# A decoder layer on one core: first down-projection operands in residual buffers, spilled residual tiles first, and the compressed branch of four heads in one exponential

## The chip, the cores and the metric

The kernel runs on one core of a Trainium2 chip. Its engines are TensorE (PE: matmuls; PEld: their weight loads), VectorE (DVE), ScalarE (ACT), GpSimd (POOL) and SyncE (SP), which issues most of the DMAs. The metric is the device time of one execution in microseconds.

## The reference

One layer over x of 1024 tokens by 1024 columns, in float32:

```
h = rms_norm(x, g_mix_norm);  z = h @ w_in            # q, 6 x k/v, gates, 3 x conv columns
per token block, kv group and head, in three branches (compressed, selected, window):
    p = masked_softmax(q.k - slope*dist);  o_branch = p @ v
attn_out = sum over branches of gate_branch * o_branch
conv_out = b_gate * conv3(c_gate * h_conv)
x = x + concat(rms_norm(attn_out), rms_norm(conv_out)) @ w_o
x = x + square(relu(rms_norm(x) @ w_up)) @ w_down     # 4096 hidden columns
```

There are 8 heads of 64 columns in 2 groups g of 4. A softmax is exp(s - max)/sum over the keys of its branch; the compressed branch has 64 keys. A float32 product is computed as three products of high and low parts (`mm3`: high·high, low·high, high·low), so each operand is split into a rounded part and the rest of it (`split`; from PSUM `split_psum`).

## The kernel before

The program first records every operation, and a planner orders them: `schedule` (L339) walks the recorded operations with estimated costs of each engine and gives every engine its own list, in which an operation with a long remaining chain goes ahead of one that was written earlier. A written-out loop is thus no order of execution, but it decides which buffers (and so which waits) an operation has. As one helper issues everything, all instructions of the profile have line L268; they are told apart by the names of their tiles.

Stages, in us of the profiled execution. **0 to 150**: norm and projections. **150 to 282**: the conv columns (`zc` banks); DVE makes the conv result `cv`, which is split into `MCh` and `MCl`, and the sums of its squares, `sqs`. Eight small matmuls `s__` of `sqs` with ones (L1013 on) then give the norm's factor `rconv`.

**282 to 340**: conv half of the output projection. The loop at L1030 goes over the eight blocks of 128 tokens in the order ORDER = 3, 2, 1, 0, 4, 5, 7, 6. For each it loads the residual of x, makes two banks `wc` of 12 matmuls and adds them, scaled by `rconv`, on DVE. The first six residual tiles stay in the ring "y" of six buffers. The last two (tokens 7 and 6) have no buffer there: they use the one buffer `xt`, which lies where `sqs` lay, and are stored to DRAM (`x1_d`) by a DMA that POOL issues. Among these matmuls stand transposes of the keys (`tp<-ident,kn`, L1028) and the queries (`qx` loaded by SP, `tpq`, `Qg`, `Qz`) and scores of the first token block.

**340 to 650**: attention, 16 pairs of token block and group. `scores` (L930) makes a head's scores in PSUM; DVE adds the distance penalty while it writes them out (`pc` for the compressed branch, `pt` for the others) and takes the extreme `nm`; ACT takes the exponential and its sum `sm`, for each head and branch in an instruction of its own; `rr` is gate over sum. `weigh` (L1073) transposes the probabilities, splits them (`ph`, `pl`) and multiplies by the values into `ot`. For each branch, in the order 1, 2, 0 (selected, window, compressed), `tail` (L1098) copies `ot` to `oTs` (ACT), transposes back into `ops` (PE), multiplies by `rr` into `ot_s` (DVE) and adds to the output `osb` (POOL). `finish` (L1146) does the attention half of the output projection (`wa` banks) and stores the sum to `x2_d`.

**650 to 957**: the up-projection in 16 pairs of hidden blocks (`pair`, L1356), by a Strassen scheme of 7 products. The squared results `d` (a tile of two halves, also in the ring "y") are put into DRAM tiles `u_d` by SP.

**957 to the end**: down-projection, L1457 on, in 8 chunks c of 2 pairs each; for a product p of 7 it loads `ur` from `u_d` (two, one for each pair), splits it into `uu` (high by ACT, low by DVE or POOL), combines and splits the weights (`we`), and runs 24 matmuls into 4 banks `X` (p = 0 to 3 accumulate in them). After each p DVE adds the four banks to residual tiles `y` in SBUF, which for chunk 0 are loaded from `x2_d` at L1475. So a matmul of p = 1 into bank `X` comes after the add of p = 0, and this after the load of `y`. The pools of `ur`, `uu` and `y` (L1432 to L1434) lie in space that the up stage's pools give back at L1429.

Of the kernel before, what the change touches and what calls it, by code (L numbers as in the profile page):

```python
# [9 lines left out]
F32 = mybir.dt.float32  # L10
F32R = mybir.dt.float32r
# [483 lines left out]
def trunk_layer(ctx, tc, x, g_mix_norm, w_in, g_q, g_k, pe_cmp, w_cmp1, b_cmp1, w_cmp2, b_cmp2,  # L495
# [341 lines left out]
    with ExitStack() as b2:  # L837
# [92 lines left out]
        def scores(tb, g, Qt, filler):  # L930
            Qg, Qz = Qt
            W = (tb + 1) * P
            WW = min(W, 640)
            nm = st.tile([P, 3, R], F32, name="nm")
            sm = st.tile([P, 3, R], F32, name="sm")
            pc = pts[g].tile([P, R, NCMP], F32, name="pc", bufs=1)
            Ps = []
            k_w = NCMP + T + W - WW
            N = NCMP + W
            cuts = [N] if N <= 512 else [320, N] if N <= 640 else [N - 512, N] if N <= 1024 else [320, N - 512, N]  # L940
            pieces = []
            c0 = 0
            for c1 in cuts:
                parts = [] if c0 else [(0, 0, NCMP, 0)]
                o = max(c0, NCMP)
                parts.append((1, o - NCMP, c1 - o, o - c0))
                pieces.append((c0, c1 - c0, parts))
                c0 = c1
            if WW == 640:
                pieces.append((k_w + 384, 256, [(2, 384, 256, 0)]))  # L950
                pieces.append((k_w, 384, [(2, 0, 384, 0)]))
            else:
                pieces.append((k_w, WW, [(2, 0, WW, 0)]))
            banks = []
            for k, n, parts in pieces:
                m = max(n, 256)
                for bank in banks:
                    if bank[0] + m <= 512:
                        break
                else:  # L960
                    bank = [0, []]
                    banks.append(bank)
                bank[1].append((k, m, bank[0], parts))
                bank[0] += m
            dtile = {0: (d_c, 56 - 8 * tb), 2: (d_sw, 512 + 640 - WW), 1: (d_sw, T - W)}
            for sl, r in enumerate(HEADS):
                sc = -(2.0 ** -(g * R + r + 1))
                pt = pts[g].tile([P, 640 + T], F32, name="pt", bufs=R)
                Ps.append(pt)
                dst = {0: pc[:, r], 2: pt[:, 0:WW], 1: pt[:, 640:640 + W]}  # L970
                seen = set()
                for _, group in banks:
                    s_ = psS.tile([P, 512], F32, name="s_")
                    for k, m, s0, _ in group:
                        nc.tensor.matmul(s_[:, s0:s0 + m], Qg[:, r], KH[g][:, k:k + m], start=True, stop=False)
                        nc.tensor.matmul(s_[:, s0:s0 + m], Qz[:, r], KL[:, k:k + m], start=False, stop=True)
                    for k, m, s0, parts in group:
                        for b, off, n, x in parts:
                            dd, d0 = dtile[b]
                            if b == 1 and d0 + off >= 512:  # L980
                                d0 += P
                            acc = nm[:, b, sl:sl + 1]
                            nc.vector.tensor_tensor_reduce(out=dst[b][:, off:off + n], in0=s_[:, s0 + x:s0 + x + n],
                                                           in1=dd[:, d0 + off:d0 + off + n],
                                                           scale=sc, scalar=acc if b in seen else 1e20,
                                                           op0=ALU.add, op1=ALU.min, accum_out=acc)
                            seen.add(b)
                for b in (1, 2, 0):
                    nc.scalar.activation(dst[b], dst[b], AF.Exp, bias=nm[:, b, sl:sl + 1],
                                         scale=-1.0, accum_out=sm[:, b, sl:sl + 1])  # L990
                for _ in range(-(-len(filler) // (R - sl))):
                    filler.pop(0)()
            rr = st.tile([P, 3, R], F32, name="rr")
            nc.vector.scalar_tensor_tensor(rr, sm, 1e-30, gates[:, tb, g], op0=ALU.max, op1=ALU.mult)
            nc.vector.reciprocal(rr, rr)
            return (Ps, pc), rr
# [30 lines left out]
        kts = [(i % 2, i // 2 % 2, i // 4) for i in range(8)]  # L1027
        for i in range(4):  # L1028
            k_transposes(*kts.pop(0))
        for it, tb in enumerate(ORDER):  # L1030
            xt = xq.tile([P, D], F32, name="xt") if it >= 6 else y_tile([P, D], f"y{tb}")
            nc.sync.dma_start(xt, x2d[tb * P:(tb + 1) * P])
            t = slice(tb * P, (tb + 1) * P)
            for nh in range(2):
                n = slice(nh * 512, (nh + 1) * 512)
                tag, bufs = (("ot", 2), ("ot", 2), ("ms", 1))[(it * 2 + nh) % 3]
                ps = psC.tile([P, 512], F32, name="wc", tag=tag, bufs=bufs)
                for c in range(4):
                    wh, wl = pieces[c]
                    mm3(ps, MCh[:, c, t], MCl[:, c, t], wh[:, 0, n], wl[:, 0, n], c == 0, c == 3)  # L1040
                nc.vector.scalar_tensor_tensor(xt[:, n], ps, rconv[:, tb:tb + 1], xt[:, n],
                                               op0=ALU.mult, op1=ALU.add)
            if it < 6:
                yacc[tb] = xt
            else:
                nc.gpsimd.dma_start(x1_d[tb * P:(tb + 1) * P], xt)
            for i in range(2):
                if kts:
                    k_transposes(*kts.pop(0))
            if it == 3:  # L1050
                Qn = queries(ORDER[0])
                first = scores(ORDER[0], 0, Qn[0], [])
# [4 lines left out]
    with ExitStack() as c_:  # L1057
# [15 lines left out]
        def weigh(tb, g, probs, rr, osb):  # L1073
# [24 lines left out]
            def tail(ot, b):  # L1098
                oTs = pq.tile([P, 512], F32, name="oTs", bufs=2)
                copy_act(oTs, ot[0])  # L1100
                ops = psC.tile([P, R, 2, HD], F32, name="ops", tag="ms", bufs=1)
                for r in range(R):
                    nc.tensor.transpose(ops[:, r].rearrange("p a d -> p (a d)"), oTs[:, r * P:(r + 1) * P], ident)
                t = pq.tile([P, R, 2, HD], F32, name="ot_s", bufs=2)
                c = rr[:, b].unsqueeze(2).unsqueeze(3).to_broadcast([P, R, 2, HD])
                tt(nc.vector, t, ops, c, ALU.mult)
                tv = t.rearrange("p (j i) a d -> p j i a d", j=2)
                if b == 1:
                    tt(nc.gpsimd, og, tv[:, :, :, 0], tv[:, :, :, 1], ALU.add)
                else:  # L1110
                    for k in range(2):
                        tt(nc.gpsimd, og, og, tv[:, :, :, k], ALU.add)
# [344 lines left out]
    for c in range(NPAIR // CHUNK):  # L1457
# [6 lines left out]
        for p in range(7):  # L1464
            ops = []
            for i, q in enumerate(qs):
                ur = eu.tile([P, 512], F32, name="ur", bufs=8)
                nc.sync.dma_start(ur, u_d[q][p])
                u = split([eU.tile([P, 512], F32R, name="uu", tag=f"u{h}", bufs=10) for h in "hl"], ur,
                          nc.gpsimd if i else nc.vector)  # L1470
                w = split(w_unit(), down_comb(Bs[i], WANT[p]), nc.vector if i else nc.gpsimd)
                ops.append((u, w))
            if c == 0 and p in (0, 1):
                for tb in range(TH[p] * 4, TH[p] * 4 + 4):
                    nc.sync.dma_start(yacc[tb], x2_d[tb * P:(tb + 1) * P])  # L1475
            ih, n = ACC[p]
            for j in range(4):
                if p == 0:
                    X[j] = bank_p("X") if j < 3 else bank_1("X")
                elif p in (4, 6):  # L1480
                    X[j] = bank_d("Z") if j % 2 else bank_e("Z")
                t = slice(j * P, (j + 1) * P)
                for i, ((uh, ul), (wh, wl)) in enumerate(ops):
                    mm3(X[j], uh[:, t], ul[:, t], wh, wl, i == 0 and p in (0, 4, 6), i == CHUNK - 1, skip_group_check=True)
                tb = TH[ih] * 4 + j
                y = yacc[tb][:, n * 512:(n + 1) * 512]
                tt(nc.vector, y, X[j], y, ALU.add)
                if c == NPAIR // CHUNK - 1 and p >= 3:
                    nc.sync.dma_start(out2d[tb * P:(tb + 1) * P, n * 512:(n + 1) * 512], y)
# [29 lines left out]
```

## Time and profile before

| | |
|---|---|
| three runs | 1276.68, 1278.77, 1284.4 us; median 1278.77 |
| the profiled execution | 1283.21 us; its span 1281.1 us, mean granted TensorE clock 0.994 |
| PE busy | 1241.3 us, 97% of the span |
| DVE, ACT, POOL busy | 896.0, 691.0, 680.0 us |

The profiled execution's own time is 2.1 us over its span. The engines' busy times overlap, so their shares don't add up to the span. The granted clock of a stretch is a mean over it: 1.00 is 2.4 GHz all the time, 0.50 would be 1.2 GHz all the time. In a list of instructions, the brackets give the engine's idle time before one and what ended it.

### The profile page before, as it was taken

Reading aid. Unit: us, or ns where it says so; the run is one execution under the profiler, and the core shown is the slowest. Engines: PE = TensorE matmul, PEld = TensorE weight load, DVE = VectorE, ACT = ScalarE, POOL = GpSimd, SP = SyncE. Lnnn points to the kernel's source line nnn. Section 1 sums busy time; section 2 is a strip of 40 time slices with the busy share of each in tenths; the row PEclk is TensorE's granted clock in tenths of the full one; section 3 lists DMA queues with packets and bytes.
Section 4 is the critical chain, followed back from the end, with each engine's and each line's share of the span. In section 5 each row is a group of like instructions: output and inputs, shape, how many; then the busy total and the mean of one; then the engine's idle time right before and its main releaser. Section 6 shows DMA issues by size and latency. Waiting matters only on the chain.

```text
span 1281.1 us, 18498 instructions
## 1 busy us (share of the span) xinstructions
PE 1241.3 (97%) x6170; PEld 1028.4 (80%) x6170; DVE 896.0 (70%) x1805; ACT 691.0 (54%) x1514; POOL 680.0 (53%) x599
## 2 busy tenths in 40 slices
PE   7999999999999999999899999999999999999998
PEld 6898888888778888888778888888877787888786
DVE  6357874333588788988884656555657988888874
ACT  7345552111589888887956455555444444444440
POOL 2245512120133422211676777777887989878860
PEclk9999999999999999999999999999999999999999
DMA  6243441202320110000315445345339655544413
GB/s 233 76 123 118 132 117 49 81 26 82 99 83 34 39 45 18 26 18 17 116 56 183 131 149 172 115 162 176 133 136 377 201 173 164 164 144 131 138 42 131
DMA packets 91575, 147.68 MB, mean 115 GB/s; under 512 B 10900, under 2 KB 45800, under 8 KB 91480
## 3 DMA queue, kind: packets, MB, share of 16 engines
q1 hardware_dynamic: 88408, 138.70, 33.7%
q10 hardware_dynamic: 2304, 5.24, 1.1%
q0 software_dynamic: 768, 2.56, 0.6%
q8 instruction: 49, 0.80, 0.3%
q14 instruction: 46, 0.38, 0.1%
HBM read 102.43 MB, written 44.04 MB: 114 GB/s over the span
## 4 chain that ended last, share of the span: by engine, by line
PE 83%; DVE 5%; DMA 4%; ACT 4%; issue 2%; POOL 1%; DVEq 0%; ACTq 0%; SPq 0%; POOLq 0%
PE X L268 23%; PE Z L268 15%; PE zc L268 10%; PE zp L268 8%; PE tp L268 6%; PE ot L268 5%; PE wa L268 3%; PE wc L268 3%; PE W L268 3%; DMA wu<-in_w_up_dram 2%; PE ops L268 1%; DVE y L268 1%; PE hp L268 1%; ACT wu L268 1%; DVE we L268 1%
## 5 line engine op out<-in xcount | busy, mean ns | idle before, releaser
L268 PE MATMUL X<-we,uu 128*128 128x512 f32 x768 | 193.1, 393 | 5.9 <-ACT uu L268 5.0
L268 PEld LDWEIGHTS X<-we,uu 128*128 128x128 f32 x768 | 144.6, 189 | 39.3 <-ACT uu L268 8.3
L268 PE MATMUL Z<-we,uu 128*128 128x512 f32 x576 | 147.6, 391 | 0.6 <-DVE y L268 0.6
L268 ACT ACTIVATE uu<-ur 128x512 fp32r<-128x512 f32 x112 | 68.9, 629 | 124.9 <-PE X L268 62.2
L268 PEld LDWEIGHTS Z<-we,uu 128*128 128x128 f32 x576 | 107.3, 188 | 26.0 <-DVE y L268 2.4
L268 PE MATMUL tp<-ident,pt 128*128 128x128 f32 x528 | 101.4, 275 | 2.3 <-ACT pt L268 1.3
L268 POOL TENSOR_TENSOR d<-d 128x512 f32<-128x512 f32 x64 | 96.3, 1525 | 12.5 <-DVE d L268 11.3
L268 DVE TENSOR_TENSOR pl<-tp,ph 128x512 fp32r<-128x512 f32 (+1 forms) x148 | 95.2, 655 | 7.5 <-ACT ph L268 7.1
L268 ACT ACTIVATE pt<-pt,nm 128x640 f32<-128x640 f32 (+7 forms) x128 | 93.8, 736 | 9.8 <-DVE nm L268 9.5
L268 ACT ACTIVATE ph<-tp 128x512 fp32r<-128x512 f32 (+1 forms) x148 | 82.9, 575 | 20.5 <-PE tp L268 14.9
L268 DVE TENSOR_TENSOR y<-X,y 128x512 f32<-128x512 f32 x128 | 79.6, 681 | 15.8 <-PE X L268 15.3
L268 ACT ACTIVATE w_hi<-w_raw,cols 128x128 fp32r<-128x128 f32 (+3 forms) x128 | 54.0, 486 | 67.4 <-PE zc L268 48.9
L268 POOL TENSOR_TENSOR uu<-ur,uu 128x512 fp32r<-128x512 f32 x56 | 78.2, 1401 | 15.2 <-DVE y L268 10.7
L268 DVE TENSOR_TENSOR we<-s,we 128x512 fp32r<-128x512 f32 x42 | 39.2, 934 | 60.0 <-ACT we L268 27.3
L268 DVE TENSOR_TENSOR uu<-ur,uu 128x512 fp32r<-128x512 f32 x56 | 65.7, 1178 | 20.7 <-ACT uu L268 19.8
L268 PEld LDWEIGHTS tp<-ident,pt 128*128 128x128 f32 x528 | 68.6, 141 | 13.6 <-ACT pt L268 2.7
L268 DVE SCALAR_TENSOR_TENSOR w_lo<-w_raw,cols,w_hi 128x128 fp32r<-128x128 f32 (+3 forms) x128 | 61.5, 525 | 24.1 <-ACT w_hi L268 23.8
L268 DVE TENSOR_TENSOR y<-Z,y 128x512 f32<-128x512 f32 x96 | 61.4, 684 | 23.7 <-PE Z L268 23.7
L268 ACT ACTIVATE wu<-wu,cols 128x256 f32<-128x256 f32 x128 | 55.4, 501 | 23.4 <-DMA wu<-in_w_up_dram 21.4
L268 POOL TENSOR_TENSOR osb<-osb,ot_s 128x256 f32<-128x256 f32 x64 | 49.2, 769 | 34.7 <-DVE ot_s L268 30.1
L268 ACT ACTIVATE we<-wu 128x512 fp32r<-128x512 f32 x57 | 35.6, 630 | 58.7 <-PE X L268 45.8
L268 PE MATMUL zc<-hTl,w_hi 128*128 128x512 f32 x192 | 65.3, 389 | 0.0
(1261 smaller groups left out, 3588.4 us busy)
## 6 DMA issues: line engine op xcount, KB each, us to landing
u_d<-d SPq DMA_DIRECT2D x112, 256.0 KB, 4.1
ur<-u_d SPq DMA_DIRECT2D x112, 256.0 KB, 2.7
wu<-in_w_up_dram SPq DMA_DIRECT2D x16, 1024.0 KB, 5.5
wd<-in_w_down_dram SPq DMA_DIRECT2D x16, 1024.0 KB, 5.8
w_raw<-in_w_in_dram SPq DMA_DIRECT2D x20, 512.0 KB, 4.0
xt<-in_x_dram SPq DMA_DIRECT2D x10, 512.0 KB, 5.2
w_raw<-in_w_cmp_dram SPq DMA_DIRECT2D x8, 512.0 KB, 4.1
q_d<-qn SPq DMA_DIRECT2D x8, 512.0 KB, 2.9
```

Source lines behind the costliest of these rows:

```text
L268: node.do.append(lambda: getattr(engine, method)(*[real(x) for x in a], **{k: real(x) for k, x in kw.items()}))
```

## The change

Three edits. First, in chunk 0 the loaded operands of p = 0 and p = 1 get other tiles: `uf`, a tile of two halves, of which the second takes the load and then the low part, the first the high part. For p = 0 these lie in the slots "x" of the pools yl and e1 (which hold weights or residual tiles earlier), for p = 1 in the ring "y". Second, the loop at L1030 takes the two blocks with the tile `xt` first, then the six others. Third, in `scores` the compressed branch leaves the loop over heads: POOL subtracts the scores of four heads from the extreme, ACT takes one exponential over 256 columns without a sum, and DVE reduces to the four sums; in `tail` for that branch ACT copies `ops` to `ot_s`, and POOL adds the two halves, multiplies by `rr` and adds to `osb`.

```diff
@@ scores
-                for b in (1, 2, 0):
+                for b in (1, 2):
                     nc.scalar.activation(dst[b], dst[b], AF.Exp, bias=nm[:, b, sl:sl + 1],
                                          scale=-1.0, accum_out=sm[:, b, sl:sl + 1])
...
+            order = "p (j i) -> p i j"
+            mx = nm[:, 0].rearrange(order, j=2).unsqueeze(3).to_broadcast([P, 2, 2, NCMP])
+            pv = pc.rearrange("p (i j) n -> p i j n", j=2)
+            tt(nc.gpsimd, pv, mx, pv, ALU.subtract)
+            nc.scalar.activation(pc, pc, AF.Exp)
+            nc.vector.tensor_reduce(sm[:, 0].rearrange(order, j=2), pv, axis=AX.X, op=ALU.add)
             rr = st.tile([P, 3, R], F32, name="rr")
@@ conv half of the output projection
-        for it, tb in enumerate(ORDER):
+        for it, tb in [*enumerate(ORDER)][6:] + [*enumerate(ORDER)][:6]:
@@ tail
                 t = pq.tile([P, R, 2, HD], F32, name="ot_s", bufs=2)
+                tv = t.rearrange("p (j i) a d -> p j i a d", j=2)
+                if b in (0,9):
+                    copy_act(t, ops)
+                    tt(nc.gpsimd, tv[:, :, :, 0], tv[:, :, :, 0], tv[:, :, :, 1], ALU.add)
+                    c = rr[:, b].rearrange("p (j i) -> p j i", j=2).unsqueeze(3).to_broadcast([P, 2, 2, HD])
+                    tt(nc.gpsimd, tv[:, :, :, 0], tv[:, :, :, 0], c, ALU.mult)
+                    tt(nc.gpsimd, og, og, tv[:, :, :, 0], ALU.add)
+                    return
@@ down-projection
-                ur = eu.tile([P, 512], F32, name="ur", bufs=8)
+                if c == 0 and p < 2:
+                    both = (y_tile([P, 2, 512], "uf") if p else (yl, e1)[i].tile([P, 2, 512], F32, name="uf", tag="x")).bitcast(F32R)
+                    u, ur = [both[:, 0], both[:, 1]], both[:, 1].bitcast(F32)
+                else:
+                    u = [eU.tile([P, 512], F32R, name="uu", tag=f"u{h}", bufs=10) for h in "hl"]
+                    ur = eu.tile([P, 512], F32, name="ur", bufs=8)
                 nc.sync.dma_start(ur, u_d[q][p])
-                u = split([eU.tile([P, 512], F32R, name="uu", tag=f"u{h}", bufs=10) for h in "hl"], ur,
-                          nc.gpsimd if i else nc.vector)
+                split(u, ur, nc.gpsimd if i else nc.vector)
```

How the planner's lists change at three places. SP's list around the boundary from up to down (`u_d_204` and `u_d_203` are the DRAM tiles of the first two pairs, `u_d_190` and `u_d_189` those of the last two, `x_d` here is `x2_d`). Before:

```order
L268 DMA u_d_189<-d 128x512
L268 DMA u_d_190<-d 128x512
L268 DMA u_d_189<-d 128x512
L268 DMA ur<-u_d_204 128x512
L268 DMA ur<-u_d_203 128x512
L268 DMA y_10073<-x_d 128x1024
L268 DMA y_10072<-x_d 128x1024
L268 DMA y_10071<-x_d 128x1024
L268 DMA y_10070<-x_d 128x1024
L268 DMA ur<-u_d_204 128x512
L268 DMA ur<-u_d_203 128x512
```

And after the change:

```order
L268 DMA u_d_190<-d 128x512 x6
L268 DMA uf<-u_d_204 128x512
L268 DMA u_d_190<-d 128x512
L268 DMA u_d_189<-d 128x512
L268 DMA uf<-u_d_203 128x512
L268 DMA y_10084<-x_d 128x1024
L268 DMA y_10083<-x_d 128x1024
L268 DMA y_10082<-x_d 128x1024
L268 DMA y_10081<-x_d 128x1024
L268 DMA ur<-u_d_204 128x512
L268 DMA ur<-u_d_203 128x512
```

The loads for p = 1 stand among the last puts of the up stage (those for p = 0 far up in the list, behind the first put of each of the first two pairs), and nothing stands between them and the loads of `y`. DVE's list at the start of the conv half of the output projection. Before:

```order
L268 TENSOR_TENSOR cv<-cv 128x512
L268 TENSOR_TENSOR sqs_1968<-sqs_1968,cv 128x512
L268 TENSOR_TENSOR KL<-tp,KH_2793 64x512
L268 TENSOR_SCALAR rs_t<-s__2825 128x8
L268 TENSOR_TENSOR KL<-tp,KH_2792 64x512
L268 TENSOR_TENSOR KL<-tp,KH_2793 64x512
L268 SCALAR_TENSOR_TENSOR y_2622<-wc,rconv,y_2622 128x512 x2
L268 SCALAR_TENSOR_TENSOR y_2801<-wc,rconv,y_2801 128x512
```

And after:

```order
L268 TENSOR_TENSOR cv<-cv 128x512
L268 TENSOR_TENSOR sqs_1968<-sqs_1968,cv 128x512
L268 TENSOR_SCALAR rs_t<-s__2825 128x8
L268 SCALAR_TENSOR_TENSOR xt<-wc,rconv,xt 128x512 x2
L268 TENSOR_TENSOR KL<-tp,KH_2793 64x512
L268 TENSOR_TENSOR KL<-tp,KH_2792 64x512
L268 TENSOR_TENSOR KL<-tp,KH_2793 64x512
L268 SCALAR_TENSOR_TENSOR y_2622<-wc,rconv,y_2622 128x512
L268 TENSOR_TENSOR KL<-tp,KH_2792 64x512
L268 TENSOR_TENSOR KL<-tp,KH_2793 64x512
L268 SCALAR_TENSOR_TENSOR xt<-wc,rconv,xt 128x512 x2
```

The adds to the first `xt` tile stand directly behind `rs_t` (which leads to `rconv`), ahead of three `KL`; those to the second come after two more `KL`. POOL's list at the first pairs of the attention. Before:

```order
L268 COPY Qz<-Qg 64x512
L268 MEMSET Qz 64x512
L268 TENSOR_TENSOR osb<-ot_s 128x2x2x64
L268 TENSOR_TENSOR osb<-osb,ot_s 128x2x2x64 x4
L268 TENSOR_TENSOR osb<-ot_s 128x2x2x64
```

And after:

```order
L268 TENSOR_TENSOR pc<-nm,pc 128x256
L268 COPY Qz<-Qg 64x512
L268 TENSOR_TENSOR osb<-ot_s 128x2x2x64
L268 MEMSET Qz 64x512
L268 TENSOR_TENSOR osb<-osb,ot_s 128x2x2x64 x2
L268 TENSOR_TENSOR ot_s<-ot_s 128x4x64
L268 TENSOR_TENSOR ot_s<-ot_s,rr 128x4x64
L268 TENSOR_TENSOR osb<-osb,ot_s 128x2x2x64
```

The subtraction for the next pair stands ahead of the current pair's sums, and the compressed branch's last two adds became three operations, of which the second needs `rr`.

## Rows read from the trace of the kernel before

**Rows 1.** The page's first part: busy time of each engine, share of the span and number of instructions.

```profile
PE 1241.3 (97%) x6170; PEld 1028.4 (80%) x6170; DVE 896.0 (70%) x1805; ACT 691.0 (54%) x1514; POOL 680.0 (53%) x599
```

**Rows 2.** Windows of the conv half's start and end and of the attention: the stretch, its length, busy time (and instructions) of PE, PEld, DVE, ACT and POOL, the granted clock, the DMA engines' share and GB/s.

```profile
290.00:295.00 5.00, 5.00 (x25) 4.37 (x26) 0.86 (x2) 1.18 (x3) 1.65 (x1) 0.69 0.63 197
340.00:345.00 5.00, 2.85 (x15) 2.30 (x14) 2.14 (x11) 2.84 (x6) 1.15 (x3) 0.81 0.61 211
345.00:350.00 5.00, 5.00 (x28) 4.40 (x28) 3.87 (x13) 4.75 (x12) 0.00 (x0) 0.85 0.37 109
350.00:630.00 280.00, 271.74 (x1710) 229.09 (x1708) 242.29 (x769) 242.81 (x622) 83.97 (x122) 1.00 0.13 45
```

**Rows 3.** The chain of waits from the last up matmul to p = 1: start, duration, what.

```profile
957.09 2.87 DMA ur<-u_d
...
959.99 0.64 ACT uu L268
...
960.67 7.33 PE X L268 x24
...
968.09 0.63 ACT we L268
...
969.29 5.73 PE X L268 x24
```

**Rows 4.** The same view later in the down-projection: 24 matmuls of one product without a break.

```profile
1015.71 5.44 PE X L268 x24
```

**Rows 5.** The window behind the boundary, with the columns of rows 2.

```profile
960.00:965.00 5.00, 4.33 (x12) 3.45 (x13) 1.44 (x2) 1.25 (x2) 5.00 (x4) 0.66 0.99 379
```

**Rows 6.** The tile `y` from 955 to 975: instructions with the duration of one in ns (least, median, most) and the first and last start; then the time from the issue of a load to its landing.

```profile
L268 SPq DMA_DIRECT2D y<-x_d x8: 319/351/647, 958.1 to 967.3; - x8
L268 DVE TENSOR_TENSOR y<-X,y x6: 680/682/692, 966.9 to 974.8; 128x512 f32<-128x512 f32 x6
...
DMA to landing us min/median/max: 7.9/8.3/8.8
```

**Rows 7.** SP's queue there: start and duration of the issues.

```profile
957.09 0.90 SPq L268 DMA_DIRECT2D ur<-u_d  x2
958.08 2.02 SPq L268 DMA_DIRECT2D y<-x_d  x4
```

**Rows 8.** The tile `xt` from 280 to 345, as in rows 6.

```profile
L268 DVE SCALAR_TENSOR_TENSOR xt<-wc,rconv,xt x4: 743/748/751, 327.4 to 338.7; 128x512 f32<-128x512 f32 x4
...
DMA to landing us min/median/max: 3.4/3.7/4.0
```

**Rows 9.** The timeline at the store of the first `xt` tile and the load of the second.

```profile
329.42 0.64 POOL L268 DMA_DIRECT2D x_d<-xt  x1 [5.58 <-DVE nm L268]
...
333.52 0.33 SPq L268 DMA_DIRECT2D xt<-in_x_dram  x1
```

**Rows 10.** The timeline at the start of the conv half of the output projection.

```profile
281.75 0.70 PE L268 MATMUL wc<-w_hi,MCh 128*128 128x512 f32 x2
...
287.65 0.69 DVE L268 TENSOR_TENSOR sqs<-sqs,cv 128x512 f32<-128x512 f32 x1
...
288.99 0.55 PE L268 MATMUL tp<-ident,kn 128*128 128x128 f32 x3 [0.68 <-DVE KL L268]
289.37 0.95 PE L268 MATMUL s__2825<-ones,sqs 128*128 128x1 f32 x8
...
296.21 1.04 PE L268 MATMUL tp<-ident,kn 128*128 128x128 f32 x8
```

**Rows 11.** The timeline of PE at its end.

```profile
342.02 0.63 PE L268 MATMUL tpq<-ident,qx 128*128 128x128 f32 x4 [1.41 <-DMA qx<-q_d]
343.40 1.11 PE L268 MATMUL tp<-ident,pt 128*128 128x128 f32 x4 [0.75 <-ACT Qg L268]
```

**Rows 12.** The groups of instructions from 340 to 660, each shape apart: busy time, mean ns of one, and the idle time before them with what ended it.

```profile
L268 PE MATMUL tp<-ident,pt 128*128 128x128 f32 x523 | 100.8, 275 | 2.3 <-ACT pt L268 1.3 <-ACT Qg L268 0.7
...
L268 POOL TENSOR_TENSOR osb<-osb,ot_s 128x256 f32<-128x256 f32 x64 | 49.2, 769 | 34.7 <-DVE ot_s L268 30.1 <-DVE rr L268 1.3 <-DVE nm L268 0.7
L268 PE MATMUL ops<-ident,oTs 128*128 128x128 f32 x192 | 36.1, 277 | 2.9 <-ACT oTs L268 1.9 <-DVE ot_s L268 0.9
...
L268 DVE TENSOR_TENSOR ot_s<-ops,rr 128x512 f32<-128x512 f32 x48 | 32.9, 685 | 4.3 <-PE ops L268 3.4 <-POOL Qz L268 0.2 <-POOL osb L268 0.2
...
L268 ACT ACTIVATE oTs<-ot 128x512 f32<-128x512 f32 x48 | 28.5, 598 | 4.8 <-PE ot L268 4.3
...
L268 ACT ACTIVATE pc<-pc,nm 128x64 f32<-128x64 f32 x60 | 20.8, 348 | 0.3 <-DVE nm L268 0.2
...
L268 ACT ACTIVATION_READ_ACCUMULATOR pc<-pc,nm 128x1 f32 x60 | 12.0, 200 | 0.0
...
L268 DVE TENSOR_TENSOR pl<-tp,ph 128x256 fp32r<-128x256 f32 x16 | 6.7, 421 | 0.1
...
L268 ACT ACTIVATE ph<-tp 128x256 fp32r<-128x256 f32 x16 | 6.2, 385 | 0.9 <-PE tp L268 0.9
...
L268 DVE SCALAR_TENSOR_TENSOR rr<-sm,gates 128x12 f32<-128x12 f32 x16 | 3.7, 230 | 1.1 <-ACT pt L268 1.1
```

**Rows 13.** The timeline of PE in chunk 0 of the down-projection: the two runs that waited for DVE.

```profile
998.59 5.88 PE L268 MATMUL Z<-we,uu 128*128 128x512 f32 x24 [0.42 <-DVE y L268]
...
1009.31 3.00 PE L268 MATMUL X<-we,uu 128*128 128x512 f32 x12 [0.53 <-DVE y L268]
```

More of the change, by code (lines that the diff above doesn't have):

```diff
@@ L1104, in tail @@
                 t = pq.tile([P, R, 2, HD], F32, name="ot_s", bufs=2)
+                tv = t.rearrange("p (j i) a d -> p j i a d", j=2)
[6 more added lines that the diff above has]
+                    return
                 c = rr[:, b].unsqueeze(2).unsqueeze(3).to_broadcast([P, R, 2, HD])
                 tt(nc.vector, t, ops, c, ALU.mult)
-                tv = t.rearrange("p (j i) a d -> p j i a d", j=2)
                 if b == 1:
```

## The prediction

> **What bounds the kernel now.** I first read the busy shares of the engines: TensorE (PE) works 1241.3 of the 1281.1 us span, 97%, and no other engine passes 70% [rows 1]. So time can come only from matmuls taken away, and the change takes none; from stretches in which PE stands idle; and from stretches in which its clock is low. The sum of all idle time is 40 us, and the question is how much of it the three edits can reach. Next come the windows of the stages the edits touch [rows 2]. In the attention stretch, 350 to 630 us, PE has 271.74 of 280, idle 8.26; ScalarE (ACT) has 242.8 and VectorE (DVE) 242.3, both below PE. In the windows around the conv half of the output projection the granted clock is 0.69 (290 to 295), 0.81 and 0.85 (340 to 350), a mixture of the levels 1.2 and 2.4 GHz. Then the chain of waits between up- and down-projection [rows 3], the one place where PE provably waits for what the first edit moves.
>
> The profiled execution took 1283.21 us; the median shown is 1278.77. I sum against 1283.21 and scale by 1278.77/1283.21 at the end.
>
> **Edit 1, first down operands, gain 3.** Before, the first u tile is loaded only when the up stage's space is free: 2.87 us of load from 957.09, 0.64 of ACT for its high part, and the first down matmul at 960.67 [rows 3]. A full-clock run of 24 such matmuls takes 5.44 [rows 4], 0.2266 each; this first run took 7.33 [rows 3], in a window with clock 0.66 [rows 5]: 1.89 lost. Then PE waits for ACT's `we`, whose issue waited for that run's start, and p=1 begins at 969.29.
>
> After, both operand pairs are loaded during the up stage, so p=0 can follow the last up matmul at about 957.5 and end at 957.5+5.44 = 963.0. But p=1 writes the bank that DVE adds to `y` after p=0, and `y` is loaded only when the space opens, at about 957.3. Before, this gate was hidden: the first `y` row came 7.9 us after its issue and the add ran at 966.9, less than 2.4 ahead of p=1 [rows 6]. After, the four `y` loads stand first on SP's queue, two `ur` loads earlier than before (the order of SP); issue times of before are 957.09 for `ur` and 958.08 for `y` [rows 7]. The nearest price for a load that is ahead of the traffic is that of `xt`, the same 512 KB, 3.4 to 4.0 [rows 8]; the nearest in this company is `y`'s own 7.9 [rows 6]. So y0 lands between 957.3+3.7 = 961.0 and 957.3+7.9 = 965.2, plus 0.68 for the add: p=1 starts between 963.0 (no wait at all) and 965.9, against 969.29. That is 6.3 to 3.4 gained. Where PE then idles 2.9 the clock may fall as it did before [rows 5], 1.9 back: 1.5 to 6.3. I take 3, nearer to `y`'s own row, since the eight `y` loads still go out together with `ur`, in a window that moves 379 GB/s [rows 5].
>
> The Trainium skill says otherwise: its page "DMA: Bandwidth & Descriptors", section "Queues, rings and completion order", gives each issuing engine's queue its own rings, in which descriptors start in order, so that what is queued behind a load should not delay it. By that rule the first `y` row would land early and the whole 6.3 would come (rival C). This trace speaks rather against it: `y`, queued behind 0.5 MB, took 7.9 or more [rows 6], where 0.5 MB at 379 GB/s [rows 5] is 1.3 us beyond `xt`'s 3.7, 5.0 in all.
>
> What the tiles cost: they lie in residual and D tiles that are free by then. The p=0 loads stand behind the first puts of the first two pairs, almost the whole up stage ahead of their use. The second p=1 load stands behind puts of pair 15 and directly ahead of `y`. Splits are the same instructions, earlier, on DVE and POOL. Zero.
>
> **Edit 2, tokens of the spilled tiles first, gain 2.8.** At the end of the conv half, the spilled tiles' reload and store no longer collide with the next query load: PE's waits 1.41 for `qx` and 0.75 for `Qg` [rows 11] go, 2.16, and with them the low clock. From 340 to 350 the clock cost between 0.15·5 = 0.75 and 0.19·5+0.75 = 1.7 [rows 2]; I take 1.2. Together −3.4.
>
> At the front, now: 0.68 idle before the key transposes [rows 10] and 0.31·5 = 1.55 by the clock [rows 2], 2.2 in all. After: PE runs the first 24 matmuls from 281.75 to 287.2; then the small `s__` sums need `sqs`, which DVE ends at 288.34 [rows 10]: 1.1 idle. The `xt` tile lies in the space of `sqs`, so its load cannot go before these sums, about 289.3: +3.7 (the median of its loads [rows 8]) + 0.75 for the add [rows 8] = 293.8; PE, with 12 matmuls (2.72) and 12 transposes (1.56 from 1.04 for 8 [rows 10]), is there at 293.6: 0.2 idle. The second tile's load waits for the store of the first: 294.5, store to reload 4.1 (329.42 to 333.52 [rows 9]), 298.6, +3.7+0.75 = 303.1; PE has 34 matmuls and 12 transposes left from 293.8, 9.3: 303.1, no idle. With the same dip of 1.55: 2.9, so +0.6. Sum −2.8; bounds −3.5 (no idle in front), and +9.4 where the two loads cost `y`'s 7.9 and bring two more dips.
>
> **Edit 3, one exponential for four heads, gain 2.** ACT loses 64 exponentials of 0.348 and 64 reads of the accumulator of 0.200, 35.1; it gains 16 of the 256-column kind, 0.385 by `ph`, and 16 copies from PSUM, 0.598 by `oTs` [rows 12]: 15.7. That is 19.4 less of 242.8 [rows 2]. DVE loses 16 multiplications of 0.685 and gains 16 reductions over 256 columns; a reduction isn't in the trace, so 0.21 (half the `pl` row) to 0.42 (the row itself): at 0.42, 4.3 less. POOL gains 32 operations of 0.769 [rows 12], 24.6 on 84.0 busy of 280 [rows 2]: covered, unless one stands in a chain (rival A). Since PE has no fewer matmuls, the gain is bounded by its idle time, 8.26; only part of its waits is on ACT (2.9 before `ops`, 2.3 before `tp`, over 340 to 660), so I take a quarter, 2; bounds −8.3 and, by rival A, +16.
>
> **Later.** Two small waits for DVE's add, 0.42 and 0.53 [rows 13], stand in chunk 0, in which the early splits leave DVE room: I take half, 0.5.
>
> Sum: −3 −2.8 −2 −0.5 = −8.3, 1274.9 beside 1283.21, **1270.5** by the median.
>
> **Rivals.**
> A, slower: the compressed chain grows. `rr`, which every tail of all branches needs, now waits for POOL's subtraction, the common exponential and a reduction, 0.77+0.39+0.42 = 1.58, where one head's exponential and read, 0.55, came last: 1.0 more in each of 16 (block, group) pairs, 16 on the path, and the 2 don't come: 1270.5+18 = 1288.5. It decides if `rr` comes later than the first tail (branch 1) wants it. For: POOL may be busy with the other pair's sums then. Against: `rr` waited only 1.1 on ACT in the whole stage [rows 12], and a pair holds some 17 us of PE work (280/16) in between. 0.12.
> B: the front of edit 2 stands in loads of 7.9 instead of 3.7: 8.4 idle and dips, 12.2 against the forecast: 1282.7. It decides if store plus load pass the 9.3 of work there. For: the clock dip at 290 coincides with 197 GB/s [rows 2]. Against: the price of store to reload is from the same pair of tiles. 0.13.
> C: `y` rows land in order and early, p=1 doesn't wait: 3.3 more, 1267; with more of the attention's idle time, 1263 to 1266. 0.15.
> D: the clock falls again at p=1 and ACT's relief lies beside matmuls: edits 1 and 3 give 1.5 and 0, 1274 to 1276. 0.10.
> Forecast, 1266 to 1274: 0.50.
>
> **Numbers.** One per cent (about what a measurement of this kernel can tell from no change) is 12.8 us: faster means below 1266.0, slower above 1291.6. Below 1266.0: half of C and a little of the forecast's edge, 0.14; above 1291.6: A with a mishap, 0.03; within: 0.83. The range from C's end to B's, 1263 to 1283, leaves out A, the tail of C and unnamed cases.
>
> **What would show it.** Right: the first down matmul within 1 us of the last up matmul; p=1's first wait on DVE's `y`, ending 5.5 to 8.5 us after the last up matmul; no wait for `qx` where the conv half ends; ACT near 223 and POOL near 109 busy in the attention's 280 us, PE idle there 5 to 7. Wrong: `ops` or `ot_s` waiting on `rr` (A); PE waits over 3 us on DVE's `xt` (B); p=1 right behind p=0 (C); a clock below 0.9 behind the boundary and 8 us idle in the attention (D).

## The result, and the profile after

The changed kernel takes 1264.51 us (median of 6 runs, 1262.25 to 1266.38) beside 1277.61 of the kernel before: ratio 0.9889, interval 0.9866 to 0.9911, faster by 13.1 us by the medians and by 14.2 by the ratio. The forecast was 1270.5, range 1263 to 1283. So the direction and the range held, and the size was low: the time is the one that rival C gave with more of the attention's idle time, 1263 to 1266, and it lies below 1266.0, which had a chance of 0.14.

The profiled execution fell from 1283.21 to 1264.10, by 19 us, more than the medians: that execution of the kernel before was 5.6 above its median, and it had low clock at 75 to 80, 290 to 295 and 340 to 350 us, where the new one has none (more on this below).

The page's first part, which answers to [rows 1]:

```profile
PE 1234.4 (98%) x6170; PEld 1023.4 (81%) x6170; DVE 902.1 (71%) x1805; ACT 683.1 (54%) x1418; POOL 708.5 (56%) x631
```

The same number of matmuls; ACT has 96 records fewer and POOL 32 more.

**The boundary.** Four views of the changed kernel there, for [rows 3, 6, 7]: the chain of waits (one row holds the last up matmul, all of p = 0 and p = 1 and the start of p = 2), PE's timeline, SP's and DVE's timelines with, in brackets, the idle time and its releaser, and the landing times of `y`.

```profile
946.83 13.38 PE X L268 x56
```

```profile
947.12 11.57 PE L268 MATMUL X<-we,uf 128*128 128x512 f32 x48
```

```profile
947.09 1.74 SPq L268 DMA_DIRECT2D y<-x_d  x4
948.88 1.25 SPq L268 DMA_DIRECT2D ur<-u_d  x2
```

```profile
951.82 1.29 DVE L268 TENSOR_TENSOR y<-X,y 128x512 f32<-128x512 f32 x2 [0.43 <-PE X L268]
...
955.58 1.89 DVE L268 TENSOR_TENSOR y<-X,y 128x512 f32<-128x512 f32 x3 [0.44 <-DMA y<-x_d]
```

```profile
DMA to landing us min/median/max: 6.3/6.7/7.1
```

48 matmuls of two products run without a break, directly behind the last up matmul. The first `y` is issued at 947.09, and its add starts at 951.82: so the load was there at most 4.7 us after its issue. And the add waited 0.43 for PE, not for the load: in the order of PE's list the first bank gets its last matmul of p = 0 as the 19th of 24, which ends at 947.12 + 18 x 0.2266 + 0.39 = 951.6. Only the fourth add waits for its load, 0.44. The view's landing times (6.3 at least) can't hold for the first tile, so they don't tell when a single tile was there; an add that ran, or waited, does.

**The conv half's start**, for [rows 8, 10]: windows, PE's timeline and the landing of `xt`.

```profile
290.00:295.00 5.00, 4.75 (x26) 3.87 (x24) 3.38 (x5) 1.69 (x3) 0.64 (x1) 1.00 0.26 105
```

```profile
291.24 0.50 PE L268 MATMUL wc<-w_hi,MCh 128*128 128x512 f32 x1 [0.25 <-DVE xt L268]
```

```profile
DMA to landing us min/median/max: 2.9/2.9/3.0
```

The whole price of the moved `xt` loads is 0.25 us of idle time, and the waits of [rows 11] are gone.

**Idle time of PE by stage.** Of every kernel, two windows of nearly the same work: the 100 us from the first conv matmul `wc`, and from there to the last `wa` matmul (columns of [rows 2]). Before and after:

```profile
281.70:381.70 100.00, 94.00 (x500) 77.32 (x499) 63.08 (x169) 50.89 (x130) 23.60 (x34) 0.97 0.30 93
381.70:650.00 268.30, 260.37 (x1626) 219.42 (x1625) 226.82 (x703) 228.68 (x576) 91.47 (x121) 1.00 0.11 37
```

```profile
279.10:379.10 100.00, 96.61 (x524) 78.71 (x523) 66.92 (x180) 50.60 (x116) 27.75 (x39) 1.00 0.28 93
379.10:637.40 258.30, 253.11 (x1594) 214.63 (x1593) 217.49 (x692) 219.77 (x492) 106.03 (x147) 1.00 0.11 39
```

Idle in the first window 6.0 and 3.4, in the second 7.9 and 5.2. (The second holds the first matmuls of the up-projection too.) The third stage is from the last up matmul to the end of the span: 1281.1 − 957.5 = 323.6 before and 1262.3 − 947.1 = 315.2 after. I use these three numbers for every experiment.

### The profile page after: what moved, and what is told of

It is laid out like the page before. It is cut to its first block, busy times and chain, and to the rows that moved or that the text cites. A ratio compares the mean times of both kernels' runs of the same rounds, so it can differ in the third digit from the quotient of the medians.

```text
span 1262.3 us, 18410 instructions
## 1 busy us (share of the span) xinstructions
PE 1234.4 (98%) x6170; PEld 1023.4 (81%) x6170; DVE 902.1 (71%) x1805; ACT 683.1 (54%) x1418; POOL 708.5 (56%) x631
## 4 chain that ended last, share of the span: by engine, by line
PE 87%; DMA 4%; ACT 4%; DVE 3%; issue 1%; SPq 0%; POOL 0%; ACTq 0%; DVEq 0%; POOLq 0%
PE X L268 24%; PE Z L268 16%; PE zc L268 10%; PE zp L268 8%; PE tp L268 6%; PE ot L268 5%; PE wa L268 4%; PE W L268 3%; PE wc L268 3%; DMA wu<-in_w_up_dram 2%; PE ops L268 1%; DVE we L268 1%; PE hp L268 1%; DVE y L268 1%; ACT wu L268 1%
## 5 line engine op out<-in xcount | busy, mean ns | idle before, releaser
L268 PE MATMUL X<-we,uu 128*128 128x512 f32 x720 | 179.2, 390 | 1.6 <-DVE y L268 1.5
L268 PEld LDWEIGHTS X<-we,uu 128*128 128x128 f32 x720 | 134.5, 188 | 31.5 <-ACT uu L268 2.2
L268 DVE TENSOR_TENSOR y<-X,y 128x512 f32<-128x512 f32 x128 | 79.8, 681 | 13.7 <-PE X L268 13.0
L268 DVE TENSOR_TENSOR uu<-ur,uu 128x512 fp32r<-128x512 f32 x54 | 69.2, 1293 | 12.5 <-ACT uu L268 11.4
L268 PEld LDWEIGHTS tp<-ident,pt 128*128 128x128 f32 x528 | 67.8, 140 | 11.8 <-PE s__4915 L268 0.6
L268 DVE TENSOR_TENSOR y<-Z,y 128x512 f32<-128x512 f32 x96 | 61.3, 683 | 21.1 <-PE Z L268 21.1
L268 PE MATMUL zc<-hTh,w_lo 128*128 128x512 f32 x192 | 65.1, 390 | 0.0
```

Source lines behind the costliest of these rows:

```text
L268: node.do.append(lambda: getattr(engine, method)(*[real(x) for x in a], **{k: real(x) for k, x in kw.items()}))
```

## The experiments

Three edits were made at once, so first each alone, and the first two together. The edits are those of the diff above: e1 has the last hunk (`uf`), e2 the second (loop order), e3 those of `scores` and `tail`, e4 the second and the last.

> The first edit alone (uf tiles for the first down operands). Theory: the two profiles show 12.2 us from the last up matmul to the first matmul of p=1 before and 5.45 after, so about 6.5 us come from this edit: 1277.6 to about 1271, no wait of the down matmuls of p=0 and p=1, granted clock 1.00 behind the boundary. Rival 'gate': the y loads land in time only by luck of the other two edits; then p=1 waits 2 to 3 us for DVE and the gain is 3 to 4: about 1274. Rival 'given back': DVE's later adds in chunk 0 wait longer by what was gained; then 1275 to 1277. Besides, this kernel's conv half is that of the kernel before: if the low clock at 290 to 295 and 340 to 350 us belongs to that order it is seen again (0.7 to 0.85); if it was chance, not.

> The second edit alone (spilled tokens first). Theory: it removes the waits for qx and Qg at the end of the conv half (2.2 us), the 0.7 at its start and the low clock there (3.3 us in the two windows): 4 to 6 us, about 1272.5. Rival 'attention order': the waits move into the attention, and the 7 us between the conv half's start and the last up matmul come from the third edit; then 1277 to 1278. Rival 'chance clock': the low clock of the one profile is not in most executions; then only the 2 to 3 us of waits, about 1275.

> The third edit alone (one exponential for four heads, tail with ACT copy and POOL). Theory: ACT has some 19 us less to do in the attention, but PE's idle time there is 8 us and only part of it waits for ACT: 2 to 3 us, about 1275. Rival 'attention order': the whole 5 to 7 us, about 1271. Rival 'longer chain': rr comes later by 1 us per pair of block and group, and without the second edit the start of the attention is crowded: 1278 to 1290, with PE waiting for DVE's rr or for ot_s.

> The first and second edits, without the third. If the parts add up (6.5 and 5): about 1266, 1.5 to 3 above the changed kernel (1264.5). If the third edit carries more (rival 'attention order'): 1269 to 1271. If the third edit costs time (rival 'longer chain'): below 1264.

| kernel | ratio to before (interval) | us, worked out | idle, 100 us from `wc` | idle, attention | last up matmul to end |
|---|---|---|---|---|---|
| before | 1 | 0 | 6.0 | 7.9 | 323.6 |
| e1, first | 0.9954 (0.9937 to 0.9972) | −5.9 | 6.2 | 8.5 | 315.8 |
| e2, second | 0.9978 (0.9966 to 0.9990) | −2.8 | 3.5 | 8.0 | 323.3 |
| e3, third | 0.9964 (0.9950 to 0.9978) | −4.6 | 6.0 | 5.2 | 323.7 |
| e4, first and second | 0.9940 (0.9925 to 0.9955) | −7.7 | 3.8 | 8.1 | 315.6 |
| all three | 0.9889 (0.9866 to 0.9911) | −14.2 | 3.4 | 5.2 | 315.2 |

(The us are ratio minus one, times the median of before in that comparison.) The parts add up: −5.9 −2.8 −4.6 = −13.3 beside −14.2, and each edit moves its own column, the others by at most 0.6; the columns fall by 2.6, 2.7 and 8.4, together 13.7. e1 decides against "gate" and "given back": p = 1 follows p = 0 there too, in the chain of waits of e1:

```profile
952.64 13.37 PE X L268 x55
```

e2 came out below its theory (4 to 6) and as its rival "chance clock" had it (2 to 3); e3 lies between its theory (2 to 3) and the rival "attention order" (5 to 7).

**e6, is it the order on SP's queue?** The changed kernel with the loads of `y` for p = 0 made less urgent for the planner:

```diff
             if c == 0 and p in (0, 1):
+                plan.plus = -8.0 if p == 0 else 0.0
                 for tb in range(TH[p] * 4, TH[p] * 4 + 4):
                     nc.sync.dma_start(yacc[tb], x2_d[tb * P:(tb + 1) * P])
+                plan.plus = 0.0
```

> The changed kernel with the four y loads of p=0 behind two ur loads and the four other y loads on SP's queue (2.5 MB ahead of them; nothing else is done differently). Theory 'queue': what stands ahead on the queue lands first, at the 400 GB/s that the window shows; the first y comes some 6 us later (2.5 MB by 400 GB/s is 6.3), p=1 waits for DVE's add by 4 to 7 us, since the add of the changed kernel ends just when p=1 needs its bank; with the clock falling after the wait, 4 to 9 us slower than the changed kernel. Rival 'shared': all loads share the engines and the order on the queue matters little: y lands at most 2 us later, 0 to 2 us slower.

It came out at 0.9913 (0.9892 to 0.9933), some 3 us slower than the changed kernel beside it (e5, below, 0.9892; the two intervals overlap), with 319.8 from the last up matmul to the end, 4.6 more. Its chain of waits at p = 1, and DVE's timeline:

```profile
952.98 0.64 ACT we L268
...
953.64 1.26 DVE we L268
954.89 0.61 DVE y L268
...
955.55 12.60 PE X L268 x41
```

```profile
955.83 0.69 DVE L268 TENSOR_TENSOR y<-X,y 128x512 f32<-128x512 f32 x1 [0.33 <-DMA y<-x_d]
```

p = 1 begins at 955.55 instead of 952.6, and the clock falls to 0.50 in the window 955 to 960. But the wait isn't quite the one I meant to make: the planner also put a `we` of DVE, which waits for ACT, ahead of the first add. Only the second add waited for its load. What the loads do can be read all the same. SP's timeline has the first two of p = 0 here, behind four other loads of `y` and two of `ur`:

```profile
947.08 0.32 SPq L268 DMA_DIRECT2D y<-x_d  x1
947.45 0.46 SPq L268 DMA_DIRECT2D y<-x_d  x1
```

The changed kernel issues these two at the same times, 947.09 and 947.46, without those six ahead. There the second was usable at most 5.0 us after its issue (its add started at 952.4 without a wait); here, by the add that waited for it, 8.4 us after. So what stands ahead on the queue delayed it by 3.4 us or more, over the 2 that "shared" allowed; that is one trace of each kernel. How much of PE's 3 us is the load's and how much that of DVE's list is not shown. In this trace p = 1 has no slack: the first add starts 3.0 us later (954.8 instead of 951.8), p = 1 starts 3.0 later, and the clock falls besides.

**e7 to e9, which half of the third edit?** e5 is the changed kernel again; e7 keeps the old `tail`, e8 the old loop of exponentials; e9 copies with another engine:

```diff
                 if b in (0,9):
-                    copy_act(t, ops)
+                    nc.vector.tensor_copy(t, ops)
```

> The changed kernel once more, for its ratio beside the others and for a second trace. If the clock of this kernel is 1.00 everywhere by its order of work, the second trace shows no window below 0.97 either; if it is chance (as the windows at 290 us of the kernels with the old and with the new order suggest), some dip may appear. Time 0.986 to 0.991 of the kernel before.

> The changed kernel with the old tail (DVE multiplies the compressed branch from PSUM, two adds on POOL); one exponential for four heads stays. ACT has 16 copies of 0.6 less, POOL 16 operations less, DVE 16 multiplications of 0.685 more. Theory 'exponential': the gain of the third edit comes from the exponentials and their reads taken off ACT: 0 to 1 us from the changed kernel either way, PE idle in the attention about 5. Rival 'tail': it comes from DVE's multiplication taken away at the end of each pair: 2 to 3 us slower, PE idle there about 8.

> The changed kernel with one exponential per head as before, and the new tail. ACT has 29 us more than the changed kernel and 10 more than the kernel before. Theory 'exponential': the gain of the third edit is gone and ACT's added copies cost besides: 3 to 6 us slower than the changed kernel. Rival 'tail': 0 to 1 us.

> The changed kernel with DVE instead of ACT making the copy of the compressed branch's ops bank; POOL still multiplies by rr. DVE has its 16 instructions of 0.6 to 0.7 us back, but they don't wait for rr. Theory 'DVE relief': the gain of the new tail comes from DVE's time and its list at the end of a pair; then the gain goes: 2 to 5 us slower than the changed kernel (0.991 to 0.993 of the kernel before), PE idle in the attention about 8. Rival 'free of rr': the gain comes from the ops bank being read without rr; then 0 to 1 us slower (0.989 to 0.990), idle about 5.

e5: 0.9892 (0.9872 to 0.9911). e7: 0.9923 (0.9902 to 0.9944). e8: 0.9886 (0.9863 to 0.9909). e9: 0.9921 (0.9902 to 0.9940). The attention windows of e7, e8 and e9, one each:

```profile
378.80:643.40 264.60, 256.08 (x1603) 215.64 (x1601) 227.04 (x710) 215.02 (x482) 99.41 (x135) 1.00 0.11 38
```

```profile
380.70:639.60 258.90, 253.26 (x1595) 215.27 (x1594) 215.77 (x683) 230.96 (x584) 98.49 (x134) 1.00 0.11 39
```

```profile
379.60:643.20 263.60, 255.52 (x1598) 215.00 (x1596) 227.14 (x710) 213.56 (x482) 106.09 (x147) 1.00 0.11 38
```

Idle time 8.5, 5.6 and 8.1. No gain of the common exponential, for which the change is named, shows here: without it (e8) the time is the same within the intervals, though ACT is busy for 231 us instead of 220. With it but without the new tail (e7), ACT falls to 215 and the time isn't shown to be better than that of e4, which has neither (0.9923 and 0.9940, intervals overlapping); PE's idle time is the old one. The gain comes with the new tail (each of e7's four runs is slower than each of e5's and e8's), and e9 narrows it: if DVE makes the same copy, which doesn't wait for `rr` either, PE's idle time is the old one and the ratio that of e7. (Its interval overlaps those of e5 and the changed kernel by a little; it is apart from that of e10, below, which has two new tails.) So it matters that ACT and not DVE reads this bank; that the reader is free of `rr` is not enough. It isn't simply DVE's sum of work either: e8 takes 16 multiplications of 0.685 off DVE [rows 12], 11.0 us, and the changed kernel, which adds 16 reductions of 0.414 (a row below), 4.3 in all, at nearly the same idle time.

**e10 to e12.** Would more of it help, and is the second edit worth as much beside the others? e10 and e12 take the new tail for the window branch too (`if b in (0, 2)`), e10 with the common exponential, e12 without; e11 is the changed kernel with the old loop order.

> The changed kernel with the new tail also for the window branch: 16 more copies of 0.6 on ACT, 16 multiplications of 0.685 less on DVE, 16 more operations on POOL. Theory 'DVE relief': DVE is close behind PE in the attention, and 11 us less of it takes another 1 to 3 us of PE's 5 us of idle time: 0.987 to 0.988 of the kernel before. Rival 'ACT next': ACT, then near 238 of 270 us, becomes what PE waits for (ops behind oTs): 0 to 3 us slower than the changed kernel.

> The changed kernel with the tokens of the spilled tiles last again. If the second edit is worth the same beside the others as alone (2.8 us by its ratio, 2.5 by PE's idle time in the first 100 us from the conv half): 2 to 4 us slower than the changed kernel, 0.991 to 0.993 of the kernel before, that idle time about 6. If the new tail already covers those waits: 0 to 1 us slower.

> As the run before with the new tail for the compressed and the window branch, but with one exponential per head again: ACT has 29 us more, some 250 of 270 us in the attention, POOL 12 less, DVE 7 less. Theory 'DVE relief': the common exponential is worth nothing as long as ACT is not what PE waits for; 0 to 1 us from the run with both (0.987 to 0.988 of the kernel before). Rival 'ACT next': with two tails on ACT its time decides, and the common exponential is what pays for them: 2 to 5 us slower (0.989 to 0.991), PE idle in the attention 7 or more, most of it behind ACT.

e10: 0.9871 (0.9851 to 0.9891). e12: 0.9878 (0.9857 to 0.9899). e11: 0.9902 (0.9883 to 0.9921). Attention windows of e10 and e12, then the first window of e11:

```profile
381.10:637.80 256.70, 251.52 (x1588) 214.31 (x1588) 211.44 (x675) 223.77 (x503) 111.11 (x159) 1.00 0.11 39
```

```profile
380.60:637.40 256.80, 250.26 (x1579) 213.17 (x1578) 206.19 (x657) 233.53 (x583) 103.64 (x146) 1.00 0.11 39
```

```profile
280.40:380.40 100.00, 94.37 (x498) 77.12 (x496) 63.45 (x170) 48.07 (x110) 27.75 (x39) 0.97 0.29 93
```

e10 has the lowest ratio of all, about 2 us below the changed kernel's, but the intervals overlap: faster than before for sure, faster than the change not shown. Its idle time in the attention is 5.2, that of the change. In e12 it is 6.5, short of the 7 the rival asked for, and the time is e10's within the intervals: this neither shows nor excludes that the common exponential begins to pay once ACT carries two tails. In e11 the 5.6 us of idle time in the first window are back, 2.2 more than in the changed kernel; by the ratio the second edit is worth 1 to 2 us there, by the idle time 2.2, alone 2.8: the same within the intervals.

## Why the prediction was right or wrong

**Edit 1, forecast 3, measured 5.9 alone (3.6 to 8.1) and 8 by the third stage's length.** p = 1 starts 5.4 us after the last up matmul (from 947.1) instead of the 11.8 of before (957.5 to 969.3): 6.3 of the 8.1 (323.6 − 315.5, the mean of e1, e4 and after) and just what the prediction had for no wait at p = 1. (The 12.2 in e1's expectation counts from the load of `ur` at 957.09.) The rest is no wait at the boundary. In the trace of before, 6.2 us lie between the last matmul and the end, against 4.9 to 5.0 in e1, e2, e3 and after: 1.2 that belong to no edit. In e2 and e3, with the old boundary, it is the clock: their 48 matmuls from p = 1 on took 13.1 and 13.0 us, where 0.2266 for each and the last one's 0.39 give 11.0. "p=0 can follow the last up matmul" held to the tenth. The step that failed is "But p=1 writes the bank that DVE adds to `y` after p=0, and `y` is loaded only when the space opens", with its price between 3.7 and 7.9 and my choice near 7.9. The gate exists, but the first load took at most 4.7. The 7.9 came from the list of landings [rows 6], and I read the late add as its proof. The trace had named another cause, in a row that I hadn't put beside it, DVE's timeline of the kernel before:

```profile
966.89 2.48 DVE L268 TENSOR_TENSOR y<-X,y 128x512 f32<-128x512 f32 x4 [5.00 <-PE X L268]
```

It waited for PE: the first bank's 19th matmul, at the low clock, ended just then. With the add's own releaser read instead of the load's landing, y's price would have been an upper bound that bound nothing, and the lower end 3.7 the nearest row.

The Trainium skill, "DMA: Bandwidth & Descriptors", section "Queues, rings and completion order", has the descriptors of a ring consumed in order on each DMA engine. By that what is issued behind a load shouldn't hold it up, though the section adds that completion doesn't follow the order of issue strictly. The trace agrees: at most 4.7 us for the first load, though three more loads of `y` and two of `ur` were issued behind it in that time; and so does e6, where loads put ahead delayed one. I had written that the trace spoke rather against the rule; it was my reading that did. Rival C, with 0.15, was the right one for this edit.

The clock's part was right: in the traces of before, e2 and e3 PE waits about 3 us ahead of p = 0 and 1.3 to 2.6 ahead of p = 1, and a window behind the first wait (before) or the second (e2, e3) has 0.66 to 0.80; in those of e1, e4 and the changed kernel there is no wait and no fall there.

**Edit 2, forecast 2.8, measured 2.8 alone (1.3 to 4.4).** Right in size, for partly other reasons. The end's waits went as forecast. In front I had 1.3 us of waits and the same dip; the trace has 0.25, since `sqs` was ready in time for the small sums and the loads took 2.9 instead of 3.7. (The bound −3.5 for no idle time in front doesn't follow from its terms, which give −4.1.) The −1.2 for the clock at the end is not shown: of the four traces with the old order two have low clock there (before, e11) and two (e1, e3) have not. The front's dip comes with both orders: 0.66 to 0.69 in three of four traces with the old one, 0.70 to 0.83 in three of ten with the new one. So what these dips cost is a matter of the execution, and a single profile doesn't price them. A window of the changed kernel, in its second trace (e5):

```profile
290.00:295.00 5.00, 5.00 (x26) 4.19 (x25) 3.18 (x5) 1.68 (x3) 0.64 (x1) 0.83 0.27 110
```

Plainer still is the stretch near 75 us, ahead of all that the edits change: up to the conv half every engine's list is the same in all these kernels. In each of the fourteen traces PE waits 1.6 to 2.3 us for a load of `ch` there, and the window 75 to 80 has 0.66 to 0.73 in six of them and 1.00 in eight. The wait and the window in e4, then in e5, which waits longer and keeps its clock:

```profile
74.61 0.63 PE L268 MATMUL tp<-ident,ch 128*128 128x128 f32 x4 [1.85 <-DMA ch<-kv_d]
75.00:80.00 5.00, 5.00 (x31) 4.98 (x28) 3.42 (x9) 3.38 (x11) 3.15 (x4) 0.66 0.09 22
```

```profile
74.92 0.63 PE L268 MATMUL tp<-ident,ch 128*128 128x128 f32 x4 [2.32 <-DMA ch<-kv_d]
75.00:80.00 5.00, 5.00 (x41) 4.96 (x42) 3.10 (x9) 3.38 (x11) 2.85 (x4) 1.00 0.23 52
```

**Edit 3, forecast 2, measured 4.6 alone (2.8 to 6.4); PE's idle time fell by 2.7.** The step that failed is "That is 19.4 less of 242.8" as the ground of a gain, and the sum was wrong too. The new operations in the changed kernel:

```profile
L268 ACT ACTIVATE pc<-pc 128x256 f32<-128x256 f32 x16 | 6.7, 419 | 1.0 <-POOL pc L268 0.9
...
L268 ACT ACTIVATE ot_s<-ops 128x512 f32<-128x512 f32 x16 | 9.7, 606 | 2.0 <-PE ot L268 1.2 <-PE ops L268 0.7
...
L268 DVE TENSOR_REDUCE sm<-pc 128x4 f32<-128x256 f32 x16 | 6.6, 414 | 2.5 <-ACT pc L268 2.4
...
L268 POOL TENSOR_TENSOR pc<-nm,pc 128x256 f32<-128x256 f32 x16 | 9.8, 615 | 67.8 <-DVE nm L268 54.8 <-DVE rs_t L268 12.7
```

Each price was near: the ACT copies cost 0.606 (forecast 0.598), the exponentials 0.419 (0.385), the reduction 0.414 (0.42), the subtraction 0.615 (0.769). But ACT's busy time fell by 7.9 in the whole execution (691.0 to 683.1), not by 19.4, and the sign "ACT near 223" did not come. The same 280 us after the change:

```profile
350.00:630.00 280.00, 272.35 (x1705) 229.51 (x1704) 237.21 (x754) 238.60 (x542) 112.99 (x160) 1.00 0.13 43
```

ACT is busy for 238.6 there; POOL, 113, came as forecast; PE's idle time is 7.65, over the 5 to 7 (the stretch holds other work than before, which is why I go by the windows above). The sum had added durations that overlap. ACT's timeline of the kernel before:

```profile
425.93 0.34 ACT L268 ACTIVATE pc<-pc,nm 128x64 f32<-128x64 f32 x1
426.16 0.19 ACT L268 ACTIVATION_READ_ACCUMULATOR pc<-pc,nm 128x1 f32 x1
426.26 0.34 ACT L268 ACTIVATE pc<-pc,nm 128x64 f32<-128x64 f32 x1
```

From one exponential to the next, with the read in between, pass 0.33 us, not 0.34 + 0.19. After the change:

```profile
419.42 0.60 ACT L268 ACTIVATE ot_s<-ops 128x512 f32<-128x512 f32 x1
419.92 0.39 ACT L268 ACTIVATE pt<-pt,nm 128x128 f32<-128x128 f32 x1
...
424.08 0.41 ACT L268 ACTIVATE pc<-pc 128x256 f32<-128x256 f32 x1
424.39 0.58 ACT L268 ACTIVATE oTs<-ot 128x512 f32<-128x512 f32 x1
```

From these starts an estimate is 64 x 0.33 = 21.1 less and 16 x (0.50 + 0.31) = 13.0 more, 8.1 in all. Nor was ACT's time what PE waited for, as e7 and e8 show: the common exponential takes 13 to 14 us off ACT's busy time (696.4 in e8, 683.1 in the changed kernel; 690.2 in e4, 676.2 in e7), and no gain shows. The small term that I wrote down for DVE's `ot_s` was the one that paid; so that this edit gained as forecast, and more, was luck as far as my reason goes. Why the step is all or nothing, 8 us of idle time in the five kernels where DVE reads all three banks with the old exponential or the new (and in e9), 5 to 6 where ACT reads one, the runs don't settle: PE's waits there are about a dozen of 0.2 to 1.6 us each, on ACT and DVE alike, and the planner reorders them all. Open is also which wait in DVE's list is the one that goes.

**Later.** I had 0.5 less for DVE's waits in chunk 0 [rows 13]; in the changed kernel one of them is 1.1:

```profile
992.61 5.72 PE L268 MATMUL X<-we,uu 128*128 128x512 f32 x24 [1.10 <-DVE y L268]
```

The other is gone, so the sum went from 0.95 to 1.10: no gain instead of 0.5.

**Rivals.** A (longer chain through POOL): `rr` needs the new chain's sums, but no run is slower for it; PE waits once for DVE's `rr`, 0.8. B (spilled reloads in front): the loads took 2.9, not 7.9; and the traffic that it named beside the dip at 290 doesn't go with the clock: e1 moved 197 GB/s there at 1.00, e10 96 at 0.70. C: right. D: wrong on p = 1, where the clock doesn't fall; its half on ACT, that the relief lies beside matmuls, fits e7 and e8, but the edit gained by its other part.

## What to carry to other kernels

When a wait is read from a trace, take the releaser of the waiting instruction and the order of what it waits for (here the 19th matmul of 24); a landing time next to it proves no wait. Before durations of one engine are added up, see whether they overlap: what an instruction costs the engine is the time from its start to the next one's (here 8 us in all instead of 19). Of a change with several parts, run the halves: the part in the headline, an exponential for four heads, gave nothing that these runs can tell, and a changed reader of one PSUM bank gave about a third of the gain. Time taken off an engine that isn't waited for bought nothing here (13 to 14 us of ACT: ratio 0.9886 without, 0.9889 and 0.9892 with).

## What the runs showed of the hardware

The first of a row of 512 KB loads on one queue was usable at most 4.7 us after its issue, though three more of its size and two of half of it were issued behind it on the same queue in that time; the fourth was waited for until 955.58, 7.2 us after its issue. The second, at most 5.0 us after its issue there, came 8.4 us after it in e6, where four of its size and two of half of it stood ahead. And the granted clock behind the same wait, in the same list of instructions, is a matter of the execution: 0.66 to 0.73 from 75 to 80 us in six of fourteen traces, 1.00 in eight. Near 290 us, with the two orders of the conv half, it is 0.66 to 0.83 in six of the fourteen and 1.00 in the others; the changed kernel has the dip in one of its two traces and not in the other.
